# The low half of the score product over 128 rows instead of 64, with an extra copy on ScalarE

## Chip, core and metric

The kernel runs on one core of one Trainium2 chip. The metric is the device time of one execution in microseconds (us); lower is better. The reader needs five engines: PE (TensorE, matrix products, with a separate row PEld for the loads of its stationary operand), DVE (VectorE), ACT (ScalarE), POOL (GpSimd) and SP, which issues the DMAs.

## What is computed

A sequence of 512 positions with 1024 features passes two layers of a first model and two layers of a second. The first model's layer (`block1`) has three mixers side by side, an mLSTM, an HGRN2 and a sliding-window attention, and then a feed-forward part and a gated embedding. The second model's layer has a mixer, a cross-attention to 256 memory vectors and a SwiGLU feed-forward part. All is float32. Cut to the scores, which the change is about:

```python
# mLSTM, chunkwise, head size 64
s = jnp.einsum('bhld,bhsd->bhls', q_, k_) * w_intra
# mixer of layer 0 of the second model: 16 heads of 64, dilated patterns
s = q @ k.T * 64 ** -0.5        # masked, softmax, times v
# mixer of layer 1: 8 heads, two scores each, softmax(s0) - lam * softmax(s1)
sc = jnp.einsum('bhcqd,bhckd->bhcqk', qblk, k, preferred_element_type=f32) * 64 ** -0.5
# sliding window attention of block1: 8 query heads share 2 key heads of 64
s = jnp.einsum('bnqhgd,bnkhd->bnhgqk', qb, kk) * 64 ** -0.5
```

## The kernel before, in words

Every float32 product is made of products of a faster type. A value `x` is split into `hi`, the value rounded to that type (ACT, `split` or a cast), and `lo = x - hi` (DVE). A GEMM step is then three matmuls in a row, `hi*hi`, `lo*hi`, `hi*lo` (`mm3`, line 817), accumulated in a bank of PSUM. Weights come by DMA as `wr` and are split into `wh` and `wl`.

The scores have heads of 64 features, half of the 128 rows over which PE sums. `q_stacks` (line 1002) makes for each head `h` one tile of 128 rows: on the head's own 64 rows `hi` of q, on the other 64 rows `lo` of q. `k_stacks` (line 1013) makes `kh`, with `hi` of k on both halves, and `kl`, with `lo` of k on the own half. One product of the q stack with `kh` over 128 rows thus gives `q_hi*k_hi + q_lo*k_hi`; a second one with `kl` over the own 64 rows adds `q_hi*k_lo`. Two functions issue this pair: `score` (line 1735), called by `attn` for the mixers of the second model (512 columns, 8 blocks of 2 heads, 4 row tiles each, in both layers: 128 pairs), and `mlstm` (line 1357), called twice in each layer of `block1` (2 heads, 4 blocks with 512, 384, 256 and 256 columns). The sliding-window attention (`swa`, line 1415) has query heads on either half that share one key head, so there `k_stacks` is called with `both=True`: DVE makes the subtraction a second time, for the other half of `kl`, and both products run over 128 rows.

The order of the work is not that of the code. The program is first recorded; `Recorder.schedule` (line 471) then plays it through with a cost for each operation and always picks, for an engine that is free, the oldest operation that is ready and whose buffers are free, weights' splits a little ahead. `emit` (line 660) issues the operations in that order, so all of them carry line L670 in the profile, and tiles have to be told by name: `kh`, `kl`, `qs` are the score's operands, `s` a bank of four for scores and some GEMMs, `g` a bank of three for GEMMs, `t` the bank for transposes and column sums. Each engine then works strictly through its list. PE's list mixes scores with GEMM steps of the heads to come. A matmul's cost in the plan goes by its columns alone, whatever its rows; a second number, that the plan uses for the clock, is scaled by the rows.

Of the kernel before, what the change touches and what calls it, by code (L numbers as in the profile page):

```python
# [10 lines left out]
F32 = mybir.dt.float32  # L11
# [3 lines left out]
ALU = mybir.AluOpType  # L15
# [3 lines left out]
P = 128  # L19
# [681 lines left out]
class Builder:  # L701
# [308 lines left out]
            out.append(s)  # L1010
        return out

    def k_stacks(self, k, both=False):

        nc = self.nc
        out = []
        for h in range(2):
            own, oth = slice(64 * h, 64 * h + 64), slice(64 - 64 * h, 128 - 64 * h)
            hi, lo = self.r("kh"), self.r("kl")
            nc.scalar.copy(hi[own], k[own])  # L1020
            nc.scalar.copy(hi[oth], k[own])
            nc.vector.tensor_tensor(lo[own], k[own], hi[own].bitcast(F32), op=ALU.subtract)
            if both:
                nc.vector.tensor_tensor(lo[oth], k[own], hi[own].bitcast(F32), op=ALU.subtract)
            out.append((hi, lo))
        return out


    def block1(self, l):
        nc = self.nc  # L1030
# [65 lines left out]
        self.swam = self.f("swam")  # L1096
        nc.sync.dma_start(self.swam, self.a["masks"])
        sw = self.swa_prep(l, lambda: fm_id(F_SK), "swk")
        ks = self.k_stacks(sw, True)
        m0 = self.mlstm(l, 0, mq[0], mk[0], tm, rows)  # L1100
        m1 = self.mlstm(l, 1, mq[1], mk[1], tm, rows)
        q = [self.swa_prep(l, lambda: fm_id(F_SQ + i), "swq") for i in range(4)]
# [254 lines left out]
    def mlstm(self, l, i, mq, mk, tm, rows):  # L1357
        nc = self.nc
        bs, col, em = rows
        qs, ks = self.q_stacks(mq), self.k_stacks(mk)  # L1360
        As = {}
        for hh in range(2):
            h = 2 * i + hh
            rb = self.sbank()
            nc.tensor.matmul(rb, self.sel[:, h:h + 1].to_broadcast([64, P]), bs, start=True, stop=True)
            w0, w1, w2 = self.f("W"), self.f("W"), self.f("W")
            W = [w0, w1[:, 0:384], w2[:, 0:256], w1[:, 384:512]]
            for j in range(4):
                nc.vector.scalar_tensor_tensor(W[j][:, 0:P], rb[:, j * P:j * P + P], col[j, j][:, h:h + 1],
                                               self.c[:, C_MNEG:C_MNEG + P], op0=ALU.add, op1=ALU.add)  # L1370
            for j in range(4):
                for ii in range(j + 1, 4):
                    o = (ii - j) * P
                    nc.scalar.activation(W[j][:, o:o + P], rb[:, ii * P:ii * P + P], AF.Exp, bias=col[j, ii][:, h:h + 1])
                nc.scalar.activation(W[j][:, 0:P], W[j][:, 0:P], AF.Exp, bias=0.0)
            kh, kl = ks[hh]
            for j in range(4):
                t0 = min(j, 2) * P
                sb = self.sbank()[:, :T - t0]
                s = slice(j * P, j * P + P)  # L1380
                nc.tensor.matmul(sb, kh[:, s], qs[hh][:, t0:], start=True, stop=False)
                own = slice(64 * hh, 64 * hh + 64)
                nc.tensor.matmul(sb, kl[own, s], qs[hh][own, t0:], start=False, stop=True)
                nc.vector.tensor_tensor(W[j], sb[:, j * P - t0:], W[j], op=ALU.mult)
                As[hh, j] = W[j]
        o = self.obank()
        for j in range(4):
            for hh in range(2):
                nc.tensor.matmul(o[64 * hh:64 * hh + 64, 128 * j:], tm["mv"](j, 64 * (2 * i + hh), 64), As[hh, j],
                                 start=j == 0, stop=j == 3)  # L1390
        y = self.f("y")
        nc.scalar.copy(y, o)
        pd = self.tbank()
        for t in range(4):
            for hh in range(2):
                for j in range(t + 1):
                    self.colsum(pd[:, 2 * t + hh:2 * t + hh + 1], As[hh, j][:, (t - j) * P:(t - j) * P + P], self.one,
                                j == 0, j == t)
        d2 = self.small(8)
        nc.scalar.activation(d2, pd[:, :8], AF.Square)  # L1400
        nc.vector.tensor_tensor(d2.rearrange("p (t h) -> p t h", h=2), d2.rearrange("p (t h) -> p t h", h=2),
                                em.rearrange("p (t h) -> p t h", h=4)[:, :, 2 * i:2 * i + 2], op=ALU.max)
        R = self.head_rms(y, d2)
        nc.vector.scalar_tensor_tensor(y, y, self.col(f"mng{l}", i), R, op0=ALU.mult, op1=ALU.mult)
        return y
# [209 lines left out]
    def attn(self, l, st):  # L1615
        nc = self.nc
# [17 lines left out]
        for i in range(8):  # L1634
# [24 lines left out]
            o = self.obank()  # L1659
            if l == 0:  # L1660
                for c2 in range(2):
                    pr = [[self.score(h, qs[h], ks[h], 2 * c2 + c, dil[2 * c2 + c]) for h in range(2)] for c in range(2)]
                    for c in range(2):
                        for h in range(2):
                            p, d = pr[c][h]
                            nc.vector.reciprocal(d, d)
                            if h == 0:
                                nc.scalar.activation(p, p, AF.Copy, scale=d)
                            else:
                                nc.vector.tensor_scalar(p, p, d, None, op0=ALU.mult)  # L1670
                    for u2 in range(2):
                        Tt = []
                        for h in range(2):
                            tb = self.tbank()
                            for u in range(2):
                                for c in range(2):
                                    a, k = (2 * u + c) * P, (2 * u2 + u) * P
                                    nc.tensor.transpose(tb[:, a:a + P], pr[c][h][0][:, k:k + P], self.ident)
                            t = self.f("T")
                            nc.scalar.copy(t, tb)  # L1680
                            Tt.append(t)
                        for u in range(2):
                            n = 2 * u2 + u
                            for h in range(2):
                                hd = ((2 * i + h) % 4) * 64
                                nc.tensor.matmul(o[64 * h:64 * h + 64, HALVES[c2]], V[n][:, hd:hd + 64],
                                                 Tt[h][:, HALVES[u]], start=n == 0, stop=n == 3)
                out.append(self.split(o))
            else:
                for c2 in range(2):  # L1690
                    Th, Tl = [self.r("Th") for _ in range(2)], [self.r("Tl") for _ in range(2)]
                    v3 = lambda t, cc: t.rearrange("p (u q) -> p u q", u=2)[:, :, cc * P:cc * P + P]
                    for cc in range(2):
                        c = 2 * c2 + cc
                        p0, d0 = self.score(0, qs[0], ks[0], c, None)
                        p1, d1 = self.score(1, qs[1], ks[1], c, None)
                        nc.vector.reciprocal(d0, d0)
                        nc.vector.reciprocal(d1, d1)
                        nc.vector.tensor_tensor(d1, d1, nlam, op=ALU.mult)
                        nc.scalar.activation(p1, p1, AF.Copy, scale=d1)  # L1700
                        nc.vector.scalar_tensor_tensor(p0, p0, d0, p1, op0=ALU.mult, op1=ALU.add)
                        tb = self.tbank()
                        for u in range(4):
                            nc.tensor.transpose(tb[:, u * P:u * P + P], p0[:, u * P:u * P + P], self.ident)
                        for h in range(2):
                            t3 = tb.rearrange("p (u q) -> p u q", u=4)[:, 2 * h:2 * h + 2]
                            nc.scalar.copy(v3(Th[h], cc), t3)
                            nc.vector.tensor_tensor(v3(Tl[h], cc), t3, v3(Th[h], cc).bitcast(F32), op=ALU.subtract)
                    for u in range(4):
                        s = slice((i % 2) * P, (i % 2) * P + P)  # L1710
                        us = slice((u % 2) * 256, (u % 2) * 256 + 256)
                        self.mm3(o[:, c2 * 256:c2 * 256 + 256], (V[u][0][:, s], V[u][1][:, s]),
                                 (Th[u // 2][:, us], Tl[u // 2][:, us]), u == 0, u == 3)
# [18 lines left out]
        self.gcyc = "gs"  # L1732
        return self.post(Weights(self, self.a[f"ao{l}"], PLANS["sq"]), out, f"mixpost{l}", (l, 9), False)

    def score(self, h, q, k, c, mask):
        nc = self.nc
        s = self.sbank()
        kh, kl = k
        nc.tensor.matmul(s, q[:, c * P:c * P + P], kh, start=True, stop=False)
        own = slice(64 * h, 64 * h + 64)  # L1740
        nc.tensor.matmul(s, q[own, c * P:c * P + P], kl[own], start=False, stop=True)
        p = self.f("P")
        mx, dn = self.small(1), self.small(1)
        if mask is None:
# [237 lines left out]
```

## Time and profile before

| | before |
|---|---|
| time, median of 3 runs | 3096.06 us (3095.2 to 3097.9) |
| the profiled execution: time, span | 3094.59 us, 3092.8 us |
| mean granted clock of PE | 0.981 |
| PE busy | 3024.8 us (98%), 16672 matmuls |
| DVE busy | 1922.2 us (62%) |
| ACT busy | 1490.9 us (48%) |

The span runs from the first to the last instruction; the time of the execution has 1.8 us around it. Matmuls overlap their neighbours, so the busy time of PE is a union of durations that are each longer than the step from one matmul to the next. The steps are read from the starts in the timeline. The granted clock is a share of 2.4 GHz; the other level is 1.2 GHz, and a number between them is a mix over time.

### The profile page before, as it was taken

What the parts mean: (1) busy time and instruction counts of PE and PEld (TensorE: products, weight loads), DVE (VectorE), ACT (ScalarE), POOL (GpSimd) and SP (SyncE); (2) the same over time, 40 slices, a digit from 0 to 9 for tenths busy, and PEclk for the clock granted to TensorE, in tenths of its full rate; (3) what the DMA queues carried; (4) which work ended last, traced back from release to release, by engine and by line L of the source; (5) the groups of instructions that cost most, each with busy time, mean ns of one, the idle gap of its engine ahead of it and who ended that gap; (6) DMA issues with size and microseconds to landing.
All of it is one profiled execution on the core that took longest, in us unless ns stands there. A gap on an engine that the chain in (4) does not pass through costs nothing.

```text
span 3092.8 us, 42875 instructions
## 1 busy us (share of the span) xinstructions
PE 3024.8 (98%) x16672; PEld 2463.1 (80%) x16672; DVE 1922.2 (62%) x3811; ACT 1490.9 (48%) x2731; POOL 75.0 (2%) x91
## 2 busy tenths in 40 slices
PE   8999999999999999999999999999999999999998
PEld 6767888887767888887776888888887778988887
DVE  7868444478878544467657756333489867653435
ACT  7557333346567333345667544222366665542223
POOL 0010000000010000000000000000000000000000
PEclk9989999999989999999999999999999999999999
DMA  3302222321312323222111423222322223332223
GB/s 119 96 12 80 102 95 96 99 91 59 106 46 63 112 96 99 98 94 77 42 55 63 125 74 102 100 97 96 102 87 71 66 65 103 97 116 96 96 98 100
DMA packets 86611, 269.96 MB, mean 87 GB/s; under 512 B 9608, under 2 KB 12680, under 8 KB 86408
## 3 DMA queue, kind: packets, MB, share of 16 engines
q1 hardware_dynamic: 86408, 267.22, 26.7%
q8 instruction: 131, 2.15, 0.3%
q14 instruction: 72, 0.59, 0.1%
HBM read 265.09 MB, written 2.10 MB: 86 GB/s over the span
## 4 chain that ended last, share of the span: by engine, by line
PE 90%; DVE 6%; ACT 2%; DMA 1%; issue 1%; POOL 0%; POOLq 0%; DVEq 0%; ACTq 0%; SPq 0%
PE s L670 47%; PE g L670 39%; PE t L670 4%; DVE wl L670 1%; DVE y L670 1%; DVE G L670 0%; ACT kh L670 0%; DVE X L670 0%; ACT wh L670 0%; DMA kr<-in_xk_dram 0%; DVE kl L670 0%; DVE B L670 0%; DMA wr<-in_w_in_tm_dram 0%; DVE x L670 0%; ACT L670 0%
## 5 line engine op out<-in xcount | busy, mean ns | idle before, releaser
L670 ACT CAST wh<-wr 128x1024 fp32r<-128x1024 f32 (+2 forms) x482 | 483.5, 1006 | 1086.0 <-PE s L670 394.3
L670 DVE TENSOR_TENSOR wl<-wr,wh 128x1024 fp32r<-128x1024 f32 (+2 forms) x482 | 560.3, 1164 | 233.8 <-ACT wh L670 226.0
L670 PE MATMUL g<-hi,wh 128*128 128x512 f32 (+1 forms) x1756 | 679.0, 387 | 12.3 <-ACT hi L670 9.3
L670 PE MATMUL g<-hi,wl 128*128 128x512 f32 (+1 forms) x1756 | 678.0, 386 | 1.5 <-DVE wl L670 1.5
L670 PE MATMUL g<-lo,wh 128*128 128x512 f32 (+1 forms) x1756 | 678.6, 387 | 0.1
L670 PE MATMUL s<-hi,wh 128*128 128x512 f32 (+1 forms) x1732 | 652.2, 377 | 2.5 <-ACT hi L670 2.4
L670 PE MATMUL s<-lo,wh 128*128 128x512 f32 (+1 forms) x1732 | 651.5, 377 | 2.0 <-DVE lo L670 2.0
L670 PE MATMUL s<-hi,wl 128*128 128x512 f32 (+1 forms) x1732 | 652.2, 377 | 0.0
L670 PEld LDWEIGHTS g<-hi,wh 128*128 128x128 f32 x1756 | 333.5, 190 | 78.9 <-ACT hi L670 10.9
L670 PEld LDWEIGHTS g<-hi,wl 128*128 128x128 f32 x1756 | 333.9, 190 | 65.4 <-issue 6.4
L670 PEld LDWEIGHTS g<-lo,wh 128*128 128x128 f32 x1756 | 333.5, 190 | 63.4 <-issue 4.9
L670 PEld LDWEIGHTS s<-hi,wh 128*128 128x128 f32 x1732 | 326.1, 188 | 62.1 <-ACT hi L670 4.1
L670 PEld LDWEIGHTS s<-lo,wh 128*128 128x128 f32 x1732 | 326.2, 188 | 60.6 <-DVE lo L670 3.1
L670 PEld LDWEIGHTS s<-hi,wl 128*128 128x128 f32 x1732 | 326.2, 188 | 57.6 <-issue 1.2
L670 ACT ACTIVATE P<-P,s 128x512 f32<-128x512 f32 (+1 forms) x224 | 137.6, 627 | 25.0 <-DVE s L670 24.4
L670 POOL TENSOR_TENSOR s<-s,mhalf 128x4 f32<-128x4 f32 (+2 forms) x53 | 69.0, 1303 | 2864.9 <-DVE s L670 2423.9
L670 ACT ACTIVATE hi<-x,cols 128x512 fp32r<-128x512 f32 (+1 forms) x112 | 73.5, 659 | 68.5 <-DVE x L670 67.8
L670 PE MATMUL t<-const,P 128*128 128x128 f32 x560 | 96.8, 281 | 1.5 <-ACT P L670 1.0
L670 PE MATMUL g<-wh,hi 128*128 128x256 f32 (+1 forms) x304 | 91.2, 301 | 0.1
L670 PE MATMUL g<-wh,lo 128*128 128x256 f32 (+1 forms) x304 | 91.1, 300 | 0.0
L670 PE MATMUL g<-wl,hi 128*128 128x256 f32 (+1 forms) x304 | 90.9, 299 | 0.0
L670 DVE TENSOR_TENSOR u<-s,R 128x512 f32<-128x512 f32 x39 | 27.0, 692 | 101.0 <-PE s L670 101.0
(300 smaller groups left out, 4058.2 us busy)
## 6 DMA issues: line engine op xcount, KB each, us to landing
wr<-in_w_down_dram SPq DMA_DIRECT2D x96, 512.0 KB, 3.3
wr<-in_gu_dram SPq DMA_DIRECT2D x88, 512.0 KB, 3.3
wr<-in_w_up_dram SPq DMA_DIRECT2D x64, 512.0 KB, 3.3
wr<-in_w_in_fm_dram SPq DMA_DIRECT2D x34, 512.0 KB, 3.3
wr<-in_qk_dram SPq DMA_DIRECT2D x32, 512.0 KB, 3.3
wr<-in_xo_dram SPq DMA_DIRECT2D x24, 512.0 KB, 3.5
wr<-in_w_down_dram SPq DMA_DIRECT2D x32, 384.0 KB, 3.2
wr<-in_w_out_dram SPq DMA_DIRECT2D x32, 256.0 KB, 2.7
```

The lines of the kernel that those rows point to most:

```text
L670: getattr(getattr(nc, o.eng), o.fn)(*[res(a) for a in o.args], **{k: res(v) for k, v in o.kw.items()})
```

## The change

`k_stacks` always fills both halves of `kl`: the own half by the subtraction on DVE as before, the other half by a copy of it on ACT. The argument `both`, and with it the second subtraction, is gone. `score` and `mlstm` run the second product over all 128 rows, with the whole of the q stack, so that it also adds `q_lo*k_lo`.

```diff
-    def k_stacks(self, k, both=False):
+    def k_stacks(self, k):
...
             nc.scalar.copy(hi[own], k[own])
             nc.scalar.copy(hi[oth], k[own])
             nc.vector.tensor_tensor(lo[own], k[own], hi[own].bitcast(F32), op=ALU.subtract)
-            if both:
-                nc.vector.tensor_tensor(lo[oth], k[own], hi[own].bitcast(F32), op=ALU.subtract)
+            nc.scalar.copy(lo[oth], lo[own].bitcast(F32))
             out.append((hi, lo))
...
-        ks = self.k_stacks(sw, True)
+        ks = self.k_stacks(sw)
...
                 nc.tensor.matmul(sb, kh[:, s], qs[hh][:, t0:], start=True, stop=False)
-                own = slice(64 * hh, 64 * hh + 64)
-                nc.tensor.matmul(sb, kl[own, s], qs[hh][own, t0:], start=False, stop=True)
+                nc.tensor.matmul(sb, kl[:, s], qs[hh][:, t0:], start=False, stop=True)
...
-    def score(self, h, q, k, c, mask):
+    def score(self, q, k, c, mask):
...
         nc.tensor.matmul(s, q[:, c * P:c * P + P], kh, start=True, stop=False)
-        own = slice(64 * h, 64 * h + 64)
-        nc.tensor.matmul(s, q[own, c * P:c * P + P], kl[own], start=False, stop=True)
+        nc.tensor.matmul(s, q[:, c * P:c * P + P], kl, start=False, stop=True)
```

The calls of `score` lose their first argument. 44 copies come onto ACT: 4 for the sliding window, 8 for the mLSTM, 32 for the two mixers. Four subtractions leave DVE. The scheduler sees the copies and makes a new order from the first of them on; among other things it has 30 loads of ACT's function tables where there were 34.

The order on ACT at the first block of the mixer of layer 0, where `z` is the k of two heads, `kh` and `kl` its stacks, `wh` the cast of a weight tile and `P` the exponential of a score. Before:

```order
L670 CAST qs_12483<-z_12451 64x512
L670 CAST wh_12492<-wr_12421 128x1024
L670 CAST kh_12522<-z_12495 64x512 x2
L670 CAST kh_12532<-z_12495 64x512 x2
L670 CAST wh_12546<-wr_12433 128x1024
L670 ACTIVATE P_12552,s_12569<-P_12552,s_12553 128x512
```

With the change:

```order
L670 CAST qs_12485<-z_12453 64x512
L670 CAST wh_12494<-wr_12423 128x1024
L670 CAST kh_12524<-z_12497 64x512 x2
L670 CAST kh_12534<-z_12497 64x512
L670 CAST kl_12530<-kl_12530 64x512
L670 CAST kh_12534<-z_12497 64x512
L670 CAST wh_12556<-wr_12435 128x1024
L670 CAST kl_12547<-kl_12547 64x512
L670 ACTIVATE P_12560,s_12580<-P_12560,s_12561 128x512
```

The copy for the first head stands between the casts of the second head, the copy for the second one behind a weight cast.

The order on PE at the same place, where `s` is a score's bank and `g` that of the GEMM which runs beside it. Before:

```order
L670 MATMUL g_12534<-hi_12044,wh_12398 128x512
L670 MATMUL s_12538<-kh_12522,qs_12478 128x512
L670 MATMUL s_12538<-kl_12528,qs_12478 128x512
L670 MATMUL s_12542<-kh_12522,qs_12478 128x512
L670 MATMUL s_12542<-kl_12528,qs_12478 128x512
L670 MATMUL s_12549<-kh_12532,qs_12483 128x512
```

With the change:

```order
L670 MATMUL g_12536<-hi_12046,wh_12400 128x512
L670 MATMUL s_12540<-kh_12524,qs_12480 128x512
L670 MATMUL s_12543<-kh_12524,qs_12480 128x512
L670 MATMUL s_12545<-kh_12524,qs_12480 128x512
L670 MATMUL s_12550<-kh_12524,qs_12480 128x512
L670 MATMUL s_12540<-kl_12530,qs_12480 128x512
L670 MATMUL s_12543<-kl_12530,qs_12480 128x512
```

Four products with `kh` of the first head now stand ahead of its first product with `kl`, and take four banks. (The sizes are those of the output, so the rows over which is summed don't show here.)

## Rows read from the trace of the kernel before

**Rows 1.** The page, chain that ended last: share of the span by engine.
```profile
PE 90%; DVE 6%; ACT 2%; DMA 1%; issue 1%; POOL 0%; POOLq 0%; DVEq 0%; ACTq 0%; SPq 0%
```

**Rows 2.** Timeline of PE, a plain GEMM: start us, us, engine, line, operation, out<-in, shapes.
```profile
1700.05 0.39 PE L670 MATMUL g<-hi,wl 128*128 128x512 f32 x1
...
1702.09 0.39 PE L670 MATMUL g<-hi,wl 128*128 128x512 f32 x1
```

**Rows 3.** Groups by shape, PE: rows*columns loaded, count | busy us, mean ns | idle before.
```profile
L670 PE MATMUL s<-kl,qs 64*128 64x512 f32 x128 | 60.6, 489 | 0.0
L670 PE MATMUL s<-kh,qs 128*128 128x512 f32 x128 | 54.6, 438 | 0.5 <-ACT P L670 0.4
```

**Rows 4.** Timeline of PE, mixer of layer 0, one half-row product between GEMM steps.
```profile
1528.90 0.28 PE L670 MATMUL s<-wh,lo 128*128 128x256 f32 x1
1529.11 0.49 PE L670 MATMUL s<-kl,qs 64*128 64x512 f32 x1
1529.53 0.39 PE L670 MATMUL s<-wl,hi 128*128 128x256 f32 x1
```

**Rows 5.** Timeline of PE, sliding window: products over 128 rows, alternately `kh` and `kl`.
```profile
233.08 0.28 PE L670 MATMUL s<-kh,qs 128*128 128x256 f32 x1
...
233.91 0.28 PE L670 MATMUL s<-kl,qs 128*128 128x256 f32 x1
```

**Rows 6.** Timeline of PEld, the weight loads at the place of rows 4.
```profile
1528.79 0.19 PEld L670 LDWEIGHTS s<-wh,lo 128*128 128x128 f32 x1
1529.11 0.18 PEld L670 LDWEIGHTS s<-kl,qs 64*128 64x128 f32 x1
1529.53 0.19 PEld L670 LDWEIGHTS s<-wl,hi 128*128 128x128 f32 x1 [0.24 <-issue]
```

**Rows 7.** Timeline of PE, mixer of layer 0, its first products.
```profile
1443.74 0.50 PE L670 MATMUL s<-kh,qs 128*128 128x512 f32 x1
1444.17 0.50 PE L670 MATMUL s<-kl,qs 64*128 64x512 f32 x1
...
1445.47 0.50 PE L670 MATMUL s<-kh,qs 128*128 128x512 f32 x1
```

**Rows 8.** Timeline of PE, mixer of layer 0, its last half-row product.
```profile
1675.99 0.49 PE L670 MATMUL s<-kl,qs 64*128 64x512 f32 x1
```

**Rows 9.** Stretches: us, busy by engine (count), PE clock, DMA share, GB/s; mLSTMs, then mixers.
```profile
155.00:200.00 45.00, 39.16 (x323) 23.49 (x320) 28.32 (x62) 29.62 (x70) 4.91 (x3) 0.70 0.03 8
858.00:900.00 42.00, 39.48 (x255) 23.82 (x255) 29.76 (x60) 27.40 (x61) 5.07 (x3) 0.72 0.13 39
1443.00:1677.00 234.00, 233.98 (x1252) 162.71 (x1251) 159.29 (x433) 161.26 (x315) 0.00 (x0) 1.00 0.16 52
2298.00:2512.00 214.00, 212.88 (x1220) 163.59 (x1220) 189.70 (x486) 146.12 (x311) 8.22 (x7) 1.00 0.17 55
```

**Rows 10.** Groups by shape, ACT and DVE: the operations that are added or removed, or like them.
```profile
L670 ACT CAST kh<-z 64x512 fp32r<-64x512 f32 x72 | 44.5, 618 | 24.3 <-DVE z L670 23.0
L670 ACT ACT_TABLE_LOAD x34 | 43.6, 1283 | 1.9 <-PEq L1972 0.7 <-DVE y L670 0.6
...
L670 DVE TENSOR_TENSOR kl<-z,kh 64x512 fp32r<-64x512 f32 x40 | 27.4, 685 | 6.2 <-ACT kh L670 5.5
```

**Rows 11.** Timeline of PE, mixer of layer 1, two of its places.
```profile
2303.19 0.50 PE L670 MATMUL s<-kl,qs 64*128 64x512 f32 x1
...
2511.43 0.49 PE L670 MATMUL s<-kl,qs 64*128 64x512 f32 x1
```

**Rows 12.** Stretches (columns PE, PEld, DVE, ACT, POOL): just ahead of the mixer of layer 1.
```profile
2250.00:2300.00 50.00, 49.10 (x381) 45.35 (x381) 46.14 (x96) 30.07 (x59) 3.27 (x3) 1.00 0.35 111
```

**Rows 13.** Timeline of PE, mLSTM of layer 0, with the idle time before and its releaser.
```profile
162.85 0.80 PE L670 MATMUL s<-qs,kh 128*128 128x512 f32 x1 [1.12 <-DVE W L670]
163.58 0.79 PE L670 MATMUL s<-qs,kl 64*128 64x512 f32 x1
```

**Rows 14.** Timeline of PE, mixer of layer 1, two half-row products together.
```profile
2416.57 0.50 PE L670 MATMUL s<-kl,qs 64*128 64x512 f32 x2
```

More of the change, by code (lines that the diff above doesn't have):

```diff
@@ L1661, in attn @@
                 for c2 in range(2):
-                    pr = [[self.score(h, qs[h], ks[h], 2 * c2 + c, dil[2 * c2 + c]) for h in range(2)] for c in range(2)]
+                    pr = [[self.score(qs[h], ks[h], 2 * c2 + c, dil[2 * c2 + c]) for h in range(2)] for c in range(2)]
                     for c in range(2):
@@ L1694, in attn @@
                         c = 2 * c2 + cc
-                        p0, d0 = self.score(0, qs[0], ks[0], c, None)
-                        p1, d1 = self.score(1, qs[1], ks[1], c, None)
+                        p0, d0 = self.score(qs[0], ks[0], c, None)
+                        p1, d1 = self.score(qs[1], ks[1], c, None)
                         nc.vector.reciprocal(d0, d0)
```

## Prediction, made before the run

> **What bounds the kernel now.** I read the chain of waits first: 90% of it is PE's [rows 1]. A busy PE says little beyond that, because matmuls overlap; what counts is how far apart their starts lie. The plain GEMM gives the yardstick: nine steps of 128-row matmuls with 512 columns take 2.04 us, so 0.227 us a step [rows 2].
>
> Next I read the groups by shape. In the two mixer layers, 128 products `s<-kl,qs` run over 64 rows and last 489 ns on average, where their full-row partners `s<-kh,qs` last 438 ns [rows 3]; the mLSTM has another 32 by the code (two layers, two calls, two heads, four blocks). With 512 columns each, a half-row product has no reason in its column count to be slower.
>
> The timeline of PE shows where it comes from. The product at 1529.11 starts 0.21 us after a 256-column matmul, and the next one follows 0.42 us later [rows 4]. Full-row 256-column products stand 0.12 us apart [rows 5] and 512-column ones 0.227 [rows 2], so going into the 64-row form costs 0.09 us there and coming out 0.19: **0.28 us a product**. The weight loads tell why: the load for the half-row product starts at 1529.11, together with its matmul, and the following full-row load also starts with its own matmul, at 1529.53 after an idle stretch, whereas the full-row matmul at 1528.90 had its load at 1528.79 [rows 4, 6]. A change between 64 and 128 rows empties the pipeline, in both directions. Where `kh` and `kl` products alternate without anything between them, each step takes 0.43 us (1443.74 to 1445.47): a pair takes 0.86 instead of 0.45, **0.41 us lost** [rows 7].
>
> That it is the rows and not the `kl` operand is visible in the same program. Sliding-window attention already uses `kl` over all 128 rows: its `kh` and `kl` products follow each other evenly, seven steps of 256 columns in 0.83 us [rows 5].
>
> **The change, part by part.**
>
> *Mixer of layer 0.* Its 64 products stand in 62 places from 1444.17 [rows 7] to 1675.99 [rows 8]. By the two prices, 62 x 0.28 = 17.4 us to 62 x 0.41 = 25.4 us; taken place by place (start before to start after, less 0.227 or 0.12 a matmul) it is 21.4 us. The stage is 234 us long and PE is busy in 233.98 of it, at the full clock of 2.4 GHz [rows 9], so time that PE saves here is saved. Added: 16 copies on ACT, at the 618 ns of the like `kh` cast [rows 10], 9.9 us. ACT has 161.3 us in 234 now [rows 9]; 171.2 in 212.6 would be 81%, so the copies lie beside PE's work. What is late next is the first `kl` product of a head: by the new order ACT runs cast, cast, cast, copy and PE four `kh` products, then four `kl`. The copy ends 4 x 0.62 = 2.5 us after the first cast began, PE reaches it after two casts and four products, 1.24 + 0.91 = 2.15 us. A wait of 0.35 us in each of 8 blocks is 2.8 us at most; I take half, 1.4. Term: **-20 us**, ends -21.4 and -16 (each of the 16 copies in the way for 0.35).
>
> *Mixer of layer 1.* 56 places with 64 products, 2303.19 among the first and 2511.43 the last [rows 11]: 16 to 23 us by the prices, 18.4 place by place. But here DVE is busy in 189.7 of 214 us [rows 9]; its subtraction for `kl` stays, so without 18.4 us it would have to be busy for 97%. The highest share in any 50 us of this trace near here is 46.14 of 50, 92% [rows 12]; at 92% the stage would shrink to 206.2 us, by 7.8. I take the middle of 7.8 and 18.4: **-13 us**, with these ends. PE's saving beyond it turns into waits on DVE.
>
> *mLSTM of both layers.* At half clock a plain step of 512 columns is 2 x 0.227 = 0.45 us (an estimate), and here the step from `kh` to `kl` takes 0.73 [rows 13]: 0.28 a change, 0.56 a product. The clock granted in these stretches is 0.70 and 0.72, a mix of 1.2 and 2.4 GHz with PE waiting often [rows 9]. With half of the products at each level: 16 x 0.56 + 16 x 0.35 = 14.6 us. PE is busy for only 39.2 of 45 and 39.5 of 42 us [rows 9], so I count 90% of it, 13. Twelve copies come onto ACT (7.4 us at 618 ns) and four subtractions of 685 ns, 2.7 us, leave DVE [rows 10]; the new order also has 30 table loads instead of 34, at 1283 ns [rows 10], two of them fewer in the mLSTM of layer 1. I let 1 us of copies show: **-12 us**. Ends: -18 (all 32 at 0.56) and +4.7 (no change was on the path; the copies are, less the subtractions).
>
> *Rest.* The scheduler rebuilt the order behind the first changed instruction, but the plain GEMM stages hold the same matmuls at 0.227 us; I cost that at nothing, and its cover is PE itself. No DMA is added; no queue of SP or POOL has a new instruction.
>
> Sum: 20 + 13 + 12 = 45 us off the profiled 3094.6, which is 3049.6. That execution lies 1.5 us under the median of 3096.1, so I forecast **3051 us**. The ends add up to -57.8 and -19.1, that is 3038 and 3077 from the median.
>
> A row against the change: at 2416.57 two half-row products of the two heads stand in one row and take 0.50 us together [rows 14], as long as one alone [rows 7]. So two of them, on the upper and lower 64 rows, ran at once, and full rows give that up: 0.227 us, here. It is in the 18.4. The Trainium skill, "TensorE: Matmul & The Clock Gate", section "Part 3: Packing small matmuls", makes this a rule: small-row matmuls in different row groups run concurrently, and that is the gain to be had. If all 64 pairs of heads stood so, full rows would cost 64 x 0.227 = 14.5 us, and 45 would become 30; the trace has one such pair, so the rule takes nothing more off here.
>
> **The rivals.**
>
> *The copies come late (slower).* PE works in order, so a `kl` product that waits holds back every GEMM product behind it, and four `kh` products ahead of it hold all four score banks. If each of the 32 copies in the mixers stood behind two casts of ACT's queue and PE waited for all three, that is 3 x 0.62 = 1.85 us each [rows 10], 59 us: 3096 - 40 + 59 = 3115. It decides from about 1.25 us a copy (40 / 32). Against it: the `kl` operand waits in the same way for DVE today, and PE's idle time before these products is 0.0 us [rows 3], because GEMM work stands between. Chance 0.04.
>
> *It is not the rows.* If a weight load could not run under a matmul that uses the same rows, a full-row `kl` would show the same steps, and the time would stay at 3096 within 2 us of copies and order. The even steps of 0.12 us speak against it [rows 5]. The Trainium skill, same page and part, says that loads overlap running matmuls only where the row groups differ; by that rule this would be the outcome, and the trace disagrees, with a full-row load 0.11 us ahead of its matmul [rows 4, 6]. Chance 0.03.
>
> *The clock comes back.* A granted clock of 0.70 over 45 us and 0.72 over 42 us [rows 9] means 27 + 23.5 us at 1.2 GHz. PE sat idle for 1.12 us just before the matmul at 162.85 and ran at half clock then [rows 13]. If full rows kept it at 2.4 GHz, up to half of those 50 us would go too: 3051 - 25 = 3026. Against it: the waits of PE on DVE `W` [rows 13] stay. Chance 0.07.
>
> *Half of it.* The mixers give only their lower ends and the new order of block1 costs a few us: 3077 to 3088. Chance 0.05.
>
> **How the numbers follow.** The forecast case, 3038 to 3077, has 0.81. Beside it lie the clock (0.07, below), the half (0.05, above), no effect (0.03) and late copies (0.04). The range from 3035 to 3077 leaves out just under 0.2. A measurement of this kernel can tell about 0.2%, 6 us, from no change: faster 0.81 + 0.07 + 0.05 = 0.93, same 0.03, slower 0.04.
>
> **What would show it.** Right: `s<-kl,qs` appears as 128*128, 0.227 us after its neighbour and with its weight load ahead of it; the mixer of layer 0 ends about 20 us sooner relative to its start, ACT near 80% there; DVE in layer 1 between 92 and 97%, with waits of PE on DVE beside it. Wrong: PE idle before `s<-kl,qs`, released by ACT `kl`, for more than 0.3 us a head; steps of 0.3 to 0.4 us that stay; or a stretch of mLSTM that got longer than before although the changes of form are gone.

## The result, and the profile after

The changed kernel takes **3046.44 us** (median of 4 runs, 3041.38 to 3049.58) against 3096.66 us before on the same chip (4 runs, 3095.2 to 3097.9): ratio 0.9836, interval 0.9819 to 0.9853, 50 us less. The forecast was 3051 us, in a range of 3035 to 3077.

The profiled execution is the fastest of its four, 3041.38 us with a span of 3039.6, so that spans differ by 53.2 us where medians differ by 50.2. Times by stage, here and below, are of single executions. The page of the kernel after, span, busy times and the chain of waits:

```profile
span 3039.6 us, 42886 instructions
...
PE 2966.9 (98%) x16672; PEld 2460.3 (81%) x16672; DVE 1912.2 (63%) x3807; ACT 1505.5 (50%) x2771; POOL 73.9 (2%) x91
...
PE 85%; DVE 8%; ACT 4%; DMA 2%; issue 1%; POOL 0%; SPq 0%; POOLq 0%; DVEq 0%; ACTq 0%
```

PE still fills 98% of its span, but its part of the chain fell from 90% [rows 1] to 85%; DVE's rose from 6 to 8, ACT's from 2 to 4. PE's busy time fell by 57.9 us, to 2966.9, with the same 16672 matmuls.

The groups by shape, after, answer to [rows 3] and [rows 10]:

```profile
L670 PE MATMUL s<-kl,qs 128*128 128x512 f32 x128 | 49.4, 417 | 1.3 <-ACT kl L670 0.5
L670 PE MATMUL s<-kh,qs 128*128 128x512 f32 x128 | 49.2, 419 | 0.1
...
L670 ACT ACT_TABLE_LOAD x30 | 38.5, 1283 | 2.0 <-DVE y L670 0.8 <-PEq L1968 0.7
...
L670 ACT CAST kl<-kl 64x512 fp32r<-64x512 f32 x44 | 27.1, 617 | 1.4 <-DVE kl L670 0.5
```

The `kl` product is a full-row one and no longer slower than its partner: 417 ns for 489, and `kh` beside it 419 for 438. The 44 copies, 617 ns each, make 27.1 us of new work on ACT.

**Where the time went.** To compare stages I mark each by the moment at which the first DMA of a weight is issued; the same weight marks the same point in both programs. The views of two weights' issues (number, KB, first and last issue), before:

```profile
L670 SPq DMA_DIRECT2D wr<-in_v_dram x16: 327/328/328, 1377.8 to 2378.4; - x16
...
L670 SPq DMA_DIRECT2D wr<-in_xq_dram x16: 327/328/328, 1695.1 to 2553.1; - x16
```

and after:

```profile
L670 SPq DMA_DIRECT2D wr<-in_v_dram x16: 327/328/328, 1362.9 to 2344.3; - x16
...
L670 SPq DMA_DIRECT2D wr<-in_xq_dram x16: 327/328/328, 1658.3 to 2502.5; - x16
```

From `v` to `xq` is the mixer of layer 0: 317.3 us before, 295.3 after (stage times are taken before rounding). So the whole program divides (us; profiled executions; the third column is the first experiment below, which has the new order but half-row products):

| stage | before | after | new order, half rows |
|---|---|---|---|
| block1, layer 0 | 290.6 | 288.2 | 293.1 |
| block1, layer 1 | 317.1 | 302.2 | 308.4 |
| behind it, up to `v` | 382.7 | 385.2 | 385.1 |
| mixer, layer 0 | 317.3 | 295.3 | 311.0 |
| cross-attention, layer 0 | 158.9 | 159.4 | 162.6 |
| mixer, layer 1 | 288.2 | 274.1 | 298.6 |
| cross-attention, layer 1 | 161.1 | 158.5 | 159.8 |

The stages that are left out differ by under 0.3 us. After against before: -22.0 and -14.1 in the two mixers, -2.4 and -14.9 in block1 (+2.5 behind it), -2.1 in the cross-attentions: -53.

**The steps.** The timeline of PE after, first block of the mixer of layer 0, answers to [rows 7] (a count above 1 merges neighbours):

```profile
1428.91 1.19 PE L670 MATMUL s<-kh,qs 128*128 128x512 f32 x4
1430.19 1.20 PE L670 MATMUL s<-kl,qs 128*128 128x512 f32 x4
1431.23 0.39 PE L670 MATMUL g<-hi,wl 128*128 128x512 f32 x1
...
1432.14 0.39 PE L670 MATMUL s<-kh,qs 128*128 128x512 f32 x1
1432.55 0.50 PE L670 MATMUL s<-kl,qs 128*128 128x512 f32 x1
1432.88 0.39 PE L670 MATMUL s<-kh,qs 128*128 128x512 f32 x1
1433.12 0.40 PE L670 MATMUL s<-kl,qs 128*128 128x512 f32 x1
1433.35 0.39 PE L670 MATMUL g<-lo,wh 128*128 128x512 f32 x1
```

The weight loads at the same place, with the idle time ahead of them and its releaser, answer to [rows 6]:

```profile
1430.19 0.76 PEld L670 LDWEIGHTS s<-kl,qs 128*128 128x128 f32 x4 [0.52 <-ACT kl L670]
...
1432.55 0.19 PEld L670 LDWEIGHTS s<-kl,qs 128*128 128x128 f32 x1 [0.45 <-ACT kl L670]
1432.89 0.19 PEld L670 LDWEIGHTS s<-kl,qs 128*128 128x128 f32 x1
1433.12 0.19 PEld L670 LDWEIGHTS g<-lo,wh 128*128 128x128 f32 x1
```

From 1432.88 the steps are 0.24 and 0.23 us, where the alternating pair of [rows 7] took 0.43 a step. The `kl` load starts at 1432.89, 0.23 us ahead of its own matmul at 1433.12 and under the `kh` matmul, which uses the same 128 rows; before, the half-row load started with its matmul [rows 6]. The two marks with `ACT kl` are the new wait: four `kh` products at 0.227 would end at 1429.82, and the first `kl` starts at 1430.19, 0.37 us late. Not all of it is the copy: the four `kh` products start at 1428.91, 1429.25, 1429.48 and 1429.71, so 0.12 us of it lies between them and 0.25 behind the last.

The stretches by engine (PE, PEld, DVE, ACT, POOL; clock, DMA, GB/s), after, answer to [rows 9]: two mLSTMs, then the two mixers:

```profile
155.00:200.00 45.00, 35.75 (x331) 25.13 (x331) 28.26 (x64) 34.55 (x81) 6.56 (x4) 0.72 0.04 11
...
858.00:900.00 42.00, 41.99 (x374) 32.32 (x371) 35.50 (x75) 37.51 (x77) 7.76 (x5) 0.88 0.11 33
...
1429.00:1635.00 206.00, 205.54 (x1211) 158.20 (x1212) 148.87 (x414) 159.40 (x313) 0.00 (x0) 1.00 0.18 57
...
2263.00:2461.00 198.00, 194.47 (x1216) 164.48 (x1215) 188.39 (x490) 153.63 (x326) 8.39 (x7) 0.99 0.18 61
```

In the mixer of layer 0 ACT is at 77% and PE is busy in 205.54 of 206 us. In layer 1 DVE is at 188.39 of 198 us, 95%. The second mLSTM got 0.88 of the clock for 0.72; the first has 0.72 for 0.70.

### The profile page after: what moved, and what is told of

It is laid out like the page before. It is cut to its first block, busy times and chain, and to the rows that moved or that the text cites. A ratio compares the mean times of both kernels' runs of the same rounds, so it can differ in the third digit from the quotient of the medians.

```text
span 3039.6 us, 42886 instructions
## 1 busy us (share of the span) xinstructions
PE 2966.9 (98%) x16672; PEld 2460.3 (81%) x16672; DVE 1912.2 (63%) x3807; ACT 1505.5 (50%) x2771; POOL 73.9 (2%) x91
## 4 chain that ended last, share of the span: by engine, by line
PE 85%; DVE 8%; ACT 4%; DMA 2%; issue 1%; POOL 0%; SPq 0%; POOLq 0%; DVEq 0%; ACTq 0%
PE s L670 44%; PE g L670 37%; PE t L670 4%; DVE wl L670 1%; DVE y L670 1%; ACT kh L670 1%; DVE z L670 1%; DVE sh L670 1%; DVE s L670 1%; DVE kl L670 1%; DVE G L670 1%; ACT wh L670 0%; DVE P L670 0%; DMA kr<-in_xk_dram 0%; DMA kr<-in_xv_dram 0%
```

## Experiments

Two theories stood first: the **rows** (the time was lost at the changes between 64 and 128 rows), and the **order** (the scheduler's new order brought most of it, which would come without full rows). Half-row products leave out `q_lo*k_lo`, as the kernel before does; so do the zeroed stacks further down. Each ratio is against the kernel before on the same chip; the groups of experiments ran on different chips, so differences between groups in us are good to a few us.

**The new order, half rows.** The order is planned as for the changed kernel and kept, copies included; only when the matmul is issued are its operands cut to the own 64 rows.

```diff
+            if o.cut is not None:
+                o.args = (o.args[0], o.args[1][o.cut], o.args[2][o.cut])
...
-        nc.tensor.matmul(s, q[:, c * P:c * P + P], kl, start=False, stop=True)
+        nc.tensor.matmul(s, q[:, c * P:c * P + P], kl, start=False, stop=True, cut=slice(64 * h, 64 * h + 64))
```

> The changed kernel's own order on every engine, row for row, with its 44 copies, but the second product of each score summed over the own 64 rows again. Theory 1 (the change between 64 and 128 rows empties PE's pipeline, and that is nearly all of the gain): about 50 us slower than the changed kernel, 3090 to 3105 us, with steps of 0.32 to 0.43 us around each half-row product as before. Theory 2 (the gain is the new order: four table loads fewer, kh products grouped): it stays with the changed kernel, 3045 to 3060 us.

Measured: 3091.64 us (10 runs, 3085.99 to 3097.47) against 3095.19; ratio 0.9982 (0.9973 to 0.9991). The order is worth 3.6 us, the rows 45 of the 50. Its groups by shape are those of [rows 3] again:

```profile
L673 PE MATMUL s<-kl,qs 64*128 64x512 f32 x128 | 58.4, 490 | 0.0
L673 PE MATMUL s<-kh,qs 128*128 128x512 f32 x128 | 52.5, 446 | 0.2 <-ACT y L673 0.2
```

And its stretches in the two mixers show a PE that is as busy over more time (206 and 198 us above):

```profile
1440.00:1661.00 221.00, 220.96 (x1209) 156.63 (x1209) 151.54 (x417) 162.80 (x315) 0.00 (x0) 1.00 0.16 53
...
2292.00:2514.00 222.00, 219.09 (x1216) 168.50 (x1214) 190.81 (x490) 154.97 (x327) 8.37 (x7) 0.95 0.17 54
```

By stage (table above, after less this kernel) the rows took 15.7 us from mixer 0, 24.5 from mixer 1 and 4.9 + 6.2 from block1. The new order as a whole saved 6.3 us in mixer 0. It groups the `kl` products there into 49 places for 62; 13 places fewer, at 0.28 to 0.41 us, are 3.6 to 5.3 us of that, and what the rest is was not tested. In mixer 1 this kernel is 10.4 us slower than the kernel before; 20 us of the stretch above ran at half clock (granted 0.95), where the kernel before had none in this stage and the changed kernel 3.4 us. This execution lies 6 us above its median, the changed kernel's 5 us below its own. So the 24.5 is too high, by up to 10 us; the kernel with the mLSTM alone in full rows, next, has half rows in mixer 1 without any half clock and takes 288.5 us, 14.4 over the changed kernel. The medians' 45 is not touched by it.

**The mixers alone, the mLSTM alone.** `k_stacks` gets an argument: `"own"` fills half of `kl`, `"both"` subtracts twice, as before. In the first kernel `mlstm` keeps its half-row product, in the second `score` does.

```diff
-        qs, ks = self.q_stacks(mq), self.k_stacks(mk)
+        qs, ks = self.q_stacks(mq), self.k_stacks(mk, "own")
...
+                nc.tensor.matmul(sb, kl[own, s], qs[hh][own, t0:], start=False, stop=True)
```

> Full rows and copies in the two mixers of the second model alone; block1 as before. Theory 1: the mixers' share, 21.9 + 14.1 us and 2.6 us behind the second, 3096 - 38 = 3058 us (3052 to 3064), and block1 at its old length. Theory 2 (the gain comes from the order of block1, which moved first): not over 20 us, 3076 to 3096 us.

> Full rows in the mLSTM alone, with copies there and for the sliding window; the mixers as before. Theory 1: the mLSTM's share, 2.4 + 12.5 us in the profiled execution of the changed kernel, 3096 - 15 = 3081 us (3076 to 3088); its two layers' shares stay as unequal as they were. Theory 2 (clock and chance of the order make block1's share): it may be anything from 3075 to 3100 us, and varies between executions by several us, as the changed kernel does (3041 to 3050).

Measured: mixers alone 3059.51 us (ratio 0.9882, 0.9864 to 0.9899), 36 us of gain; mLSTM alone 3076.24 (0.9935, 0.9917 to 0.9952), 19. Their sum is 55 us for 50 together (52 in the changed kernel's second timing, below). By stage the first has 298.3 and 274.9 us in the mixers and 317.4 in block1 of layer 1, the second 314.3, 288.5 and 300.0. The parts add up to within 3 to 5 us.

**The other half by DVE.** The copy is replaced by a second subtraction.

```diff
-            nc.scalar.copy(lo[oth], lo[own].bitcast(F32))
+            nc.vector.tensor_tensor(lo[oth], k[own], hi[own].bitcast(F32), op=ALU.subtract)
```

> Full rows everywhere, but the other half of kl is made by a second subtraction on DVE (685 ns) instead of a copy on ACT (618 ns). Theory 1 with DVE as the next limit in the mixer of layer 1: 16 subtractions of 0.685 us, 11 us, come onto an engine that is busy over 90% there, so 3046 + 3 to 11 = 3049 to 3057 us, the loss in that mixer alone. Rival (the copies on ACT are what PE now waits for): 3038 to 3046 us.

Measured: 3065.74 us (0.9900, 0.9885 to 0.9915), 19 more than with the copy on ACT and 9 beyond the range of the first theory. Mixer 1 takes 284.1 us for 274.1, and PE is idle for 11 us of its stretch:

```profile
2275.00:2487.00 212.00, 200.98 (x1235) 168.94 (x1233) 202.49 (x512) 147.35 (x316) 7.46 (x7) 0.98 0.17 57
```

DVE fills 202.49 of 212 us, again 95.5%. Sixteen subtractions of 685 ns are 11 us; the stage grew by 10, as the theory of DVE as the next limit has it, though the order is a new one here too. Block1 of layer 1 lost another 12.9, which I did not expect: the order differs there, and the whole program has 32 table loads for 30.

**Table loads.** Half of what block1's layer 1 gained came with the order (317.1 to 308.4 in the table), and the new order has fewer loads of ACT's tables. Two kernels try that alone. The first is the kernel before, with the second sine of that layer moved right behind the first, which saves two loads; the second is the changed kernel with an exponential between the two sines, which adds two.

```diff
+        order.remove(c)
+        order.insert(order.index(s) + 1, c)
...
+        order.remove(e)
+        order.insert(i + 1, e)
```

> The kernel before, with one instruction moved: in block1 of layer 1 the second of the two sine activations stands right behind the first on ACT, so that two table loads (2.6 us of ACT) go. Theory A (the part of block1's gain that is not the rows, 9 us in layer 1, comes from the table loads between the exponentials of the mLSTM): 3095 - 5 to 9 = 3086 to 3090 us. Theory B (it is the rest of the new order): 3092 to 3096 us.

> The changed kernel, with one instruction moved the other way: in block1 of layer 1 an exponential stands between the two sines, so that two table loads come back. Theory A: 3046 + 5 to 13 = 3051 to 3059 us, the loss in that block. Theory B: 3045 to 3050 us.

Measured: the first 3092.45 us (0.9987, 0.9978 to 0.9997), 4 us off, while its block1 of layer 1 took 317.0 us in the profile, no less; the second 3048.15 (0.9839, 0.9825 to 0.9854), with 306.3 us there for 302.2 (300.1 in another execution of the changed kernel). Two loads are worth nothing by the first and 4 to 6 of those 9 us by the second.

The clock changed with the order too. Stretches of 50 us in block1 of layer 1, before:

```profile
860.00:910.00 50.00, 47.75 (x366) 30.87 (x367) 35.16 (x72) 34.30 (x76) 6.71 (x4) 0.73 0.09 26
```

the new order with half rows:

```profile
860.00:910.00 50.00, 48.36 (x406) 34.69 (x405) 38.42 (x81) 39.84 (x85) 7.19 (x5) 0.90 0.09 28
```

and after:

```profile
860.00:910.00 50.00, 49.99 (x419) 39.45 (x420) 40.20 (x85) 40.65 (x83) 8.88 (x5) 0.90 0.11 33
```

The granted clock is 0.90 with either kind of product and 0.73 in the old order; between 850 and 950 us 30.7 us ran at 1.2 GHz before, 13.7 in both others. Up to half of those 17 us, 8.5, is what the clock could give back, about the 8.7 that the order took from this stage. That the clock is the cause is not shown, and two other kernels speak against it as the only one. Over the whole stage the clock was 0.92 in 317.1 us before, 0.94 in 308.4 us in the new order with half rows and 0.95 in 302.2 us after. The kernel with the second subtraction on DVE has the clock of the changed kernel and nearly the time of the kernel before, with PE idle for 28 us of the stage (19 both before and after):

```profile
676.00:991.10 315.10, 286.72 (x1867) 221.22 (x1866) 260.65 (x672) 204.43 (x464) 21.15 (x15) 0.95 0.21 65
```

The last kernel below (zeros, with `bs,sel`) has nearly the clock of the kernel before and is 10 us shorter:

```profile
672.20:979.30 307.10, 282.74 (x1850) 221.56 (x1849) 257.09 (x665) 202.48 (x464) 19.13 (x18) 0.93 0.21 67
```

So where the 8.7 us of the order come from stays open.

**Each copy twice.** Every `kl` copy of the changed kernel is issued a second time right behind the first, all else in the same order.

```diff
+            if o.eng == "scalar" and o.fn == "copy" and o.args[0].tile is o.args[1].tile:
+                order.append(o)
```

> The changed kernel's order, with each of the 44 copies on ACT issued twice, one right behind the other. If the copies lie beside PE's work: 3046 + 0 to 6 us. If they are on the path (each score's second product waits for ACT): 44 x 0.62 = 27 us, 3066 to 3075 us, with PE idle before the kl products, released by ACT kl.

Measured: 3066.64 us (0.9900, 0.9885 to 0.9914). 44 copies of 0.617 us are 27 us more on ACT, and 20 of them show. Groups by shape of this kernel, the row of the product:

```profile
L670 PE MATMUL s<-kl,qs 128*128 128x512 f32 x128 | 49.6, 419 | 15.8 <-ACT kl L670 15.8
```

PE stands idle ahead of the `kl` products for 15.8 us, all of it released by `ACT kl`, where the single copy leaves 1.3, 0.5 of it released by `ACT kl`. The cover under which the copies cost nothing is thinner than one copy.

**Half rows in pairs.** Here `score` takes both heads and issues their two half-row products, on the upper and the lower 64 rows, one behind the other; no copies in the mixers. The Trainium skill ("TensorE: Matmul & The Clock Gate", section "Part 3: Packing small matmuls") advises this: small-row matmuls in different row groups run concurrently. The mLSTM has full rows.

```diff
+        for h in range(2):
+            nc.tensor.matmul(s[h], q[h][:, c * P:c * P + P], k[h][0], start=True, stop=False)
+        for h in range(2):
+            own = slice(64 * h, 64 * h + 64)
+            nc.tensor.matmul(s[h], q[h][own, c * P:c * P + P], k[h][1][own], start=False, stop=True, pair=h)
```

> Half rows again in the mixers, without copies there, but the half-row products of the two heads always stand next to each other; the mLSTM as in the changed kernel. If the two run at once on their own rows and a pair pays for one change in and one out: two kh products and a pair take 2 x 0.227 + 0.1 + 0.227 + 0.2 = 0.98 us against 4 x 0.227 = 0.91 for full rows, 64 x 0.07 = 5 us over the changed kernel, 3048 to 3054 us. If they run one after the other: 64 x 0.3 = 19 us over it, 3062 to 3070 us. If each still pays for itself: 3076 us, as with full rows in the mLSTM alone.

Measured: 3061.18 us (0.9883, 0.9868 to 0.9897), 15 more than with full rows, between the first two forecast ranges. It is 15 less than with full rows in the mLSTM alone, where each half-row product pays for itself. Timeline of PE, one pair in mixer 1:

```profile
2333.21 0.40 PE L673 MATMUL s<-kh,qs 128*128 128x512 f32 x1
2333.53 0.50 PE L673 MATMUL s<-kl,qs 64*128 64x512 f32 x2
2333.96 0.38 PE L673 MATMUL g<-lo,kh 128*128 128x256 f32 x1
```

The group by shape, with a busy time that was 60.6 us when the products stood alone [rows 3]:

```profile
L673 PE MATMUL s<-kl,qs 64*128 64x512 f32 x128 | 32.5, 504 | 0.0
```

Two products take 0.50 us together, as in [rows 14], so they do run at once; but the last `kh` and the pair take 0.75 us (2333.21 to 2333.96), and with the other `kh` at 0.227 it is 0.98 us for four products. Four full-row steps are 4 x 0.227 = 0.91. The concurrency of that rule is there, and the two changes of form cost a little more than it gives: 64 x 0.07 = 5 us. The other 10 us are not in the steps. By stage, mixer 0 takes 303.9 us for 295.3 and the cross-attention behind it 154.5 for 159.4; the two together, 458.4 for 454.7, fit 32 x 0.07 = 2.2 roughly, mixer 0 by itself does not. Mixer 1 takes 290.0 for 274.1, far more; there PE is idle for 10.4 us of the stretch (3.5 of 198 with full rows), and DVE is at 89%:

```profile
2265.00:2481.00 216.00, 205.61 (x1230) 161.37 (x1230) 191.94 (x491) 146.98 (x314) 7.67 (x7) 0.97 0.17 56
```

In this stage 13.7 us ran at 1.2 GHz, 3.4 with full rows, which is up to 5 us more. A pair needs the stacks of both heads at once; whether that makes the wait is not tested.

**Zeros for the copy.** The products run over 128 rows, but the other half of `kl` is zeroed once in four tiles that are kept for it (two general tiles fewer for that), and 40 copies go. The second kernel also runs the 8 products `bs,sel`, which have 64 rows, over 128.

```diff
-            hi, lo = self.r("kh"), self.r("kl")
+            hi, lo = self.r("kh"), self.r("kl") if both else self.kz[self.kn % 2][h]
...
-            nc.tensor.matmul(rb, self.sel[:, h:h + 1].to_broadcast([64, P]), bs, start=True, stop=True)
+            nc.tensor.matmul(rb, self.sel[:, h:h + 1].to_broadcast([P, P]), bs, start=True, stop=True)
```

> Full rows without the 40 copies of mLSTM and mixers: kl lies in four fixed tiles whose other half is set to zero once, so the second product adds q_hi*k_lo alone, as before the change; the sliding window keeps its 4 copies; the pool of general tiles has 56 instead of 58. If the copies cost nothing as long as the plan knows of them (PE waits 0.5 us on them in the changed kernel): 3042 to 3050 us, with new order in block1 worth up to 10 us either way. If they are worth as much as their doubling cost (20 us): 3025 to 3035 us.

> The same, and the eight products of the mLSTM that spread bs over all columns, the last ones over 64 rows, run over 128 rows too, with zeros in the other half. By the price of a change of rows (0.28 to 0.56 us): 2 to 4 us less than the kernel with zeroed halves, less what the wider set-up of bs costs on POOL (some 1 us a layer). If the order of block1 decides: anything from -8 to +8 us.

The changed kernel ran beside them once more:

> The changed kernel itself, once more, beside the two: 3041 to 3050 us.

Measured, all on one chip against 3093.94 us: zeros 3047.27 (0.9843, 0.9829 to 0.9858), zeros with `bs,sel` 3044.46 (0.9842, 0.9825 to 0.9858), the changed kernel 3042.10 (0.9833, 0.9818 to 0.9848). The three can't be told apart. Without copies mixer 0 takes 292.8 us for 295.3 and block1 of layer 1 308.7 for 300.1: where the copies show, in mixer 0, they cost about 2.5 us, and block1 takes more than that back; that its new order does it is argued, not shown. No version beat the changed kernel.

## Why the prediction was right

*The price of a change of form.* It stood on the steps of [rows 2], [rows 4] and [rows 7], 0.28 to 0.41 us a product. With the same order and only the rows changed, 45 us came back from 160 products, 0.28 us each on average, and the 49 places of mixer 0 gave 15.7 us, 0.32 each: the reading of the steps holds. The rival that loads can't run under a matmul on the same rows is refuted by the load at 1432.89. The Trainium skill ("TensorE: Matmul & The Clock Gate", section "Part 3: Packing small matmuls") lists as what overlaps only loads for other row groups, though the same section also lets a load into a background weight buffer go ahead. By the first rule alone the steps would have stayed at 0.43; here they are 0.24.

*Mixer of layer 0, forecast -20 (-21.4 to -16).* Measured -22.0, just beyond the end: 15.7 by the rows and 6.3 by the new order, of which the grouping of `kl` products explains 3.6 to 5.3. The price counted the old order's 62 places; the grouping, which the order's rows showed, was used only for the wait that it causes. That wait was forecast at 0.35 us a block, and is 0.37 at the first, 0.25 of it behind the last `kh`; with zeros for the copies, in another order, the stage was 2.5 us shorter, near the 2.8 that I gave as the most.

*Mixer of layer 1, forecast -13 (-18.4 to -7.8).* Measured -14.1, with DVE at 95%, between the 92 and 97% that the term was made from. That DVE is close to the limit is borne out by the second subtraction: 11 us on DVE, 10 us of stage. But the -13 was the middle of a wide range, so that it came so near is in part luck, and the term held nothing for the copies: with zeros in their place the stage took 272.1 and 272.7 us in two kernels, for 274.1, so some 2 of the 4.3 us that are missing from 18.4 are theirs. Waits of PE's loads, before and after, in this stage (idle us, count, longest):

```profile
PEld s L670 <- issue: 16.3, 60, 0.4
```

```profile
PEld s L670 <- ACT kl L670: 3.6, 8, 0.7
```

The 60 stalls of loads for the `s` bank are gone, and the new order with half rows has 57 of them, so it is the full rows that end them; eight waits for the copy are what is new.

*mLSTM, forecast -12 (-18 to +4.7).* The total holds (-2.4 and -14.9, or -12.4 with the 2.5 us that the stage behind gave back: 14.8 in all), but **the step failed in its split.** I spread the gain evenly over both layers, all by changes of form. Layer 0 gave 2.4; it runs at 0.72 of the clock, 0.70 before, and PE is idle for 9.3 us of the 45, 5.8 before, so part of the time saved on PE became waits. Layer 1 gave 14.9, of which 8.7 came with the order. The rows gave 4.9 + 6.2 = 11 us against the new order with half rows, near the 12, only because that order had lost 2.5 in layer 0 first; that the total met the forecast is in part luck.

*The clock comes back, chance 0.07.* It did so in part, in layer 1 (47.8 us at 1.2 GHz in that stage before, 30.7 after). The new order with half rows has 34.1 there, so most of it came with the order and not with full rows as the rival had it.

*Late copies, chance 0.04.* They were not late, but nearly: one more copy of 0.617 us each would have taken 20 of the 50 us back. I had put the deciding point at 1.25 us a copy for the mixers' gain; what I did not say is that the cover is under 0.62.

*Rest, forecast 0.* -2.1 in the cross-attentions, within the scatter: the one of layer 0 took 159.4 and 162.4 us in two executions of the same changed kernel. Its four times spread over 8 us; those of the kernel before spread over 3 in four executions here, but over 10 (3092.43 to 3102.35) in thirteen beside the table-load kernels, so the changed kernel does not scatter more.

## What to carry to other kernels

Read steps between starts, not durations or the busy share: a matmul over half of the rows that stands alone among full-row ones costs more than a full one, and filling the other half, with a copy or with zeros, is worth it where PE is the bound and another engine has time. Pairing half-row products leaves little of the loss in the steps, but of the 30 us that full rows in the mixers are worth beyond full rows in the mLSTM it gained 15 here. And price a change that goes through a scheduler twice, at its old and its new order: the order alone went with changes of 6 to 10 us in single stages, in both directions, and 3.6 us in sum.

## What the runs showed that I had not expected

The granted clock changed with the order of the same half-row products: in block1 of layer 1 47.8 us ran at 1.2 GHz in the old order and 34.1 in the new, and in the mixer 1 stretch of the new order 20 us where the old order ran none (and full rows 3.4). The time of the stage did not follow it in every kernel. Two concurrent half-row products plus the two changes of form cost 0.98 us with their partners, 0.07 more than four full-row steps, so in the steps the two effects nearly cancel.
